# One triangular substitution for four delta-rule heads, heads run in two groups of four, and an order maker that repeats its passes with mean times

## The chip, the cores and the metric

The kernel runs on one core of a Trainium2 chip. Its time is that of one execution on the device, in microseconds. A core has five engines with instruction streams of their own: TensorE (PE; its weight loads are listed as PEld), VectorE (DVE), ScalarE (ACT), GpSimd (POOL) and SyncE (SP), which here issues the DMA transfers. They wait for one another by semaphores.

## The reference

One layer of a trunk, then a last RMSNorm; 1 x 1024 frames of 1024 features, 256 memory tokens, all float32. The delta-rule branch has 8 heads of 128 and works in chunks:

```python
h = rmsnorm(x, norm_mix_g); proj = h @ w_in        # all heads' columns at once
# branch A, gated DeltaNet, per head and chunk:
gc = jnp.cumsum(g, axis=-1)
decay = jnp.exp(jnp.where(incl, gc[..., :, None] - gc[..., None, :], -jnp.inf))
kk = jnp.einsum('bhnid,bhnjd->bhnij', k, k)
lower = jnp.where(strict, beta[..., :, None] * kk * decay, 0.0)
sol = triangular_solve(lower, [beta * v, beta * exp(gc) * k], lower=True, unit_diagonal=True)
a_qk = jnp.einsum('bhnid,bhnjd->bhnij', q, k) * decay
# scan over the chunks: delta = u - w S; o = q_dec S + a_qk delta; S = g_end S + k_dec^T delta
y_a = (rmsnorm(o) * silu(z)) @ w_branch_gdn
# branch B, GLA, 4 heads, gives y_b
x = x + (sigmoid(gate_a) * y_a + sigmoid(gate_b) * y_b) @ w_out
x = x + cross_attention(rmsnorm(x), rmsnorm(mem))  # 4 heads
x = x + relu(rmsnorm(x) @ w1)**2 @ w2
return rmsnorm(x, norm_final_g)
```

q, k and v pass a causal convolution of 4 taps and SiLU; q and k are l2-normalised.

## The kernel before

**Dense work.** Each float32 operand is split into a high and a low part (ScalarE rounds it, L622; VectorE or GpSimd subtracts, L623), and a product is made of three: high by high, high by low, low by high (L582, L584, L586). Large matrices go through a seven-product block scheme whose sums are the tiles A0a, A0b, A1a, A1b and B0a to B1b. One product has mostly 128 x 512 results. `wop`, `whi`, `wlo` are split weights and `raw` the weights as loaded.

**Phases.** First K and V of the memory, the norm of x (the factors `rs_o` are transposed at L679) and gates; then four GLA heads, between which the q, k, v columns of the delta-rule heads are projected, convolved (L1275) and stored in DRAM (`gd`, in the profile `gdq`, `gdk`, `gdv`, `gdz`); then the delta-rule phase; then gates, branch projections and merge, attention, MLP and the last norm.

**Delta-rule phase** (`phase_gdn`). The 8 heads run in 4 pairs. `near` loads a pair's k and, in `gdn_keys`, transposes it (L654, eight blocks for a head) for the norms and for `kd`, the keys times their decay (tile kdt, L1345). `gdn_decay` makes the matrix `dm` of a head from its cumulated gates: a load, a mask on GpSimd, a subtraction (L1326) and an exponential (L1327). `gdn_gram` multiplies k by itself (L1369) and makes `NT`, the negated strictly triangular matrix of a chunk. `gdn_subst` inverts its 32 x 32 diagonal blocks: ScalarE copies the blocks into the tile X (L1412), VectorE transposes (L1418), then 31 steps on VectorE or GpSimd make a product `pr` and add it to `Pm` (L1425, L1427), two transposes follow (L1429, L1431), and the results are copied to `PF` and `subPT`. X holds 32 columns; two heads of 8 blocks fill 16, the other 16 are set to zero. `gdn_inverse` joins the blocks to the inverse of the whole chunk on TensorE (L1449, L1458). `gdn_queries` makes q times k (L1386), `gdn_v` loads v and multiplies it (L1471), `gdn_scan` runs over the chunks (L1485, L1494, L1511) and writes its outputs over v, `gdn_out` transposes v (L654), multiplies by the SiLU of z (tile sz) and stores to `oad`. Pair p+1's keys, Gram products and substitution are written before pair p's scan. The v tiles of even and odd pairs have tags of their own (v0, v1), two buffers each.

**What fills and what orders.** Dense work (the z projections, numbered gates, the attention's folded weights Q0 to Q3 and O0 to O3) is pushed to a queue by `others(FILL[..])`, and `fill(n)` lets n of its steps into the program between steps of a head. But the order of the program is not the last word. The class `Plan` takes all instructions, gives each a cost, and makes a list schedule: `latest` works out by when each has to be done, `forward` places them; on TensorE the earlier in the program goes first of those that are ready, on other engines the one due earliest. Some operations may go to VectorE or GpSimd, as free. `make` repeats the two passes `ROUNDS` times (1 before) and keeps the order whose end is earliest by its own costs. `sooner(gen, SOON)` marks instructions as due SOON ns earlier. The buffers have fixed places (`LAYP`, `LAYQ`: tag, bytes, buffers).

Of the kernel before, what the change touches and what calls it, by code (L numbers as in the profile page):

```python
# [18 lines left out]
P = 128  # L19
D = 1024  # L20
T = 1024
NB = 8
# [18 lines left out]
FA, FB, FC, FD, FE, FG, FH, FI = 23, 31, 30, 20, 47, 24, 1, 0  # L41
# [6 lines left out]
EV = (('K2', 1, 'x0'), ('K3', 1, 'kk'), ('V0', 4, 'x1'), ('V1', 1, 's0'), ('V1', 12, 'n0'), ('V2', 12, 's1'), ('V3', 1, 'kv'), ('V3', 4, 'n1'))  # L48
# [18 lines left out]
EXTRA = (('k', 'v', 't', 'q'), ('v', 't', 'k', 'q'), ('v', 't', 'k', 'q'), ('v', 't', 'k', 'q'))  # L67
QB, FOLDB = 2, 1
SFILL, PFILL, TFILL = 4, (2, 12), (4, 14, 0, 8, 10, 10)
FILL = ((7,), ('z0', 6, 10, 'z6', 'Q2'), (9, 'O1', 'z5', 'Q3', 'z1'), ('z2', 'z4', 14, 'z3', 'O0', 11, 13, 'O3', 'Q0', 8, 'Q1'), ('z7', 'O2', 12))  # L70
LASTG = (15, 5)
LAYP = (('PF', 8192, 1), ('k1', 4096, 2), ('NT1', 4096, 2), ('NT0', 4096, 2), ('Pm', 4096, 1), ('dm', 4096, 2), ('k0', 4096, 2), ('kdt0', 4096, 2), ('kdt1', 4096, 2), ('pr', 1024, 1), ('q', 4096, 2))
LAYQ = (('AT', 4096, 2), ('v0', 4096, 2), ('acc', 2048, 2), ('sz', 2048, 2), ('v1', 4096, 2), ('X', 4096, 2))
OUT = "out_0_dram"
HOLD, MARGIN = 0, 0
SOON = 0
ROUNDS, TOP, PAD, WINDOW, LOAD, HORIZON, LAND, RATE = 1, 228656, 128, 3413, 1283, 30000, 2600, 300
# [100 lines left out]
class Plan:  # L178
# [252 lines left out]
    def make(self):  # L431
# [69 lines left out]
class Layer:  # L501
# [507 lines left out]
    def push_pair(self, sp, x, after=None):  # L1009
# [8 lines left out]
        def done(i, half, o, x_):  # L1018
            nc.scalar.activation(o, x_, AF.Silu)
            nc.sync.dma_start(self.gd["z", u][i][:, half * HALF:(half + 1) * HALF], o)  # L1020
# [171 lines left out]
    def queue_gla(self):  # L1192
# [5 lines left out]
        for h in range(LH):  # L1198
# [3 lines left out]
            q += [[a[f"w_g{x}"][h] if len(x) == 1 else a["w_gz"][int(x[1])]]  # L1202
# [132 lines left out]
    def gdn_keys(self, sp, sq, heads):  # L1335
# [3 lines left out]
        for e, (h, st) in enumerate(heads):  # L1339
            kd = st["kd"] = self.til(sp, [P, NB, P], f"kdt{h // 2 % 2}", bufs=2)  # L1340
            for g in range(2):
                gs = slice(4 * g, 4 * g + 4)
                pt = self.transpose4([st["k"][:, 4 * g + i, :] for i in range(4)])
                self.sumsq(sq, pt, ss[:, e, gs])
                nc.vector.tensor_tensor(kd[:, gs, :], c3(pt), self.kf[:, gs, h:h + 1].broadcast_to([P, 4, P]), MUL)  # L1345
                yield
        v, b, nb, vs = (self.til(sq, [P, 2, NB], t, bufs=2) for t in ("vv", "b", "nb", "vs"))
# [56 lines left out]
    def gdn_subst(self, sp, sq, sts):  # L1404
# [3 lines left out]
        nc.gpsimd.memset(C[:, :, 16:32], 0.0)  # L1408
# [22 lines left out]
        nc.vector.transpose(t2, Pm.rearrange("p i j -> p j i"))  # L1431

        PT, PF = self.subPT, self.til(sp, [P, 16, P], "PF", bufs=1)
        nc.gpsimd.memset(PF, 0.0)
        for b in range(4):
            q = slice(32 * b, 32 * b + 32)
            nc.scalar.activation(PF[q, :, q].rearrange("p u i -> p i u"), t2[q, :, 0:16], AF.Copy)
            nc.vector.tensor_copy(PT[q, :, q].rearrange("p u i -> p i u"), t1[q, :, 0:16])
# [130 lines left out]
    def phase_gdn(self, wp):  # L1569

        nc, a = self.nc, self.a
        with ExitStack() as ctx:
# [30 lines left out]
            def near(p):  # L1603
                for e, (h, st) in enumerate(heads(p)):
                    st["k"] = self.til(sp, [P, NB, P], f"k{p % 2}", bufs=2)
                    self.load(st["k"].rearrange("p a b -> p (a b)"), self.gd["k", p][e])
                yield from self.gdn_keys(sp, sq, heads(p))
# [9 lines left out]
            self.gdn_cols(sq)  # L1617
# [852 lines left out]
```

## Time and profile before

| what | value |
|---|---|
| median of 3 runs | 2115.37 us (2114.18 to 2116.24) |
| the profiled execution | 2115.5 us |
| its span in the profile | 2113.8 us |
| TensorE busy | 2091.5 us, 99% |
| VectorE busy | 1595.6 us, 75% |
| ScalarE busy | 1208.1 us, 57% |
| GpSimd busy | 152.2 us, 7% |
| delta-rule phase (first key transposes to last v transposes) | 673.8 to 1042.8 us |

The profile takes one execution. The busy time of an engine is the time in which it runs an instruction; matmuls are pipelined, so that each row of a matmul is longer than the spacing of two. Busy shares are means over stages with different limits: a stage is read from what its engines waited for. In a timeline, a row has start, duration, engine, line, operation, tiles and, in brackets, how long the engine had been idle and what released it. "x8" is a run of eight alike.

### The profile page before, as it was taken

The page shows a single profiled execution, that of the slowest core. Times are in us where ns is not written, and L with a number is a line of the kernel's source. Part 1 is how long each engine was busy: PE and PEld are TensorE (multiplying, and loading weights), DVE is VectorE, ACT ScalarE, POOL GpSimd, SP SyncE. Part 2 cuts the span into 40 slices and gives each one's busy share as a digit, 9 for nine tenths or more (in the row PEclk, how much of TensorE's full clock was granted, in tenths as well). Part 3 has the DMA queues.
Part 4 walks back from the last instruction along what each step waited for, and adds up shares of the span by engine and source line. Part 5 has one row for each costly group of instructions (what it writes and reads, how often), then busy time and mean ns, then how long its engine had stood idle before and what let it go on. Part 6 is the DMA issues. An engine that isn't in the chain of part 4 may idle for free. (4 is left out here: it accounts for less than half of the span.)

```text
span 2113.8 us, 30953 instructions
## 1 busy us (share of the span) xinstructions
PE 2091.5 (99%) x10938; PEld 1780.5 (84%) x10938; DVE 1595.6 (75%) x2830; ACT 1208.1 (57%) x2391; POOL 152.2 (7%) x174
## 2 busy tenths in 40 slices
PE   8999999999999999999999999999999999999998
PEld 8889887898888899889888888888788888888887
DVE  7858887948876888787569899469967567567855
ACT  7456666536646586765655456565755557444433
POOL 0000000001001223311000000000100000000000
PEclk9999999999999999999999999999999999999999
DMA  8322232312325444555586752226444446678852
GB/s 329 130 72 62 91 105 64 113 61 96 100 93 194 131 129 139 168 176 162 176 278 239 257 169 80 90 79 218 137 145 140 160 151 219 212 249 278 269 175 100
DMA packets 158363, 329.57 MB, mean 156 GB/s; under 512 B 17016, under 2 KB 25720, under 8 KB 158208
## 3 DMA queue, kind: packets, MB, share of 16 engines
q1 hardware_dynamic: 158064, 327.57, 47.1%
q8 instruction: 86, 1.41, 0.3%
q14 instruction: 69, 0.57, 0.1%
q10 hardware_dynamic: 144, 0.03, 0.0%
HBM read 227.36 MB, written 100.17 MB: 155 GB/s over the span
## 5 line engine op out<-in xcount | busy, mean ns | idle before, releaser
L622 ACT ACTIVATE wop<-raw 128x512 fp32r<-128x512 f32 (+1 forms) x520 | 336.6, 653 | 406.4 <-PE pd L586 179.5
L623 DVE TENSOR_TENSOR wop<-raw,wop 128x512 fp32r<-128x512 f32 (+1 forms) x494 | 347.3, 707 | 209.3 <-ACT wop L622 206.4
L582 PE MATMUL pd<-t,wop 128*128 128x512 f32 x332 | 130.4, 393 | 0.9 <-ACT t L622 0.9
L586 PE MATMUL pd<-t,wop 128*128 128x512 f32 x332 | 130.9, 394 | 0.0
L584 PE MATMUL pd<-t,wop 128*128 128x512 f32 x332 | 130.7, 394 | 0.0
L584 PE MATMUL pd<-A1b,wop 128*128 128x512 f32 x272 | 106.1, 390 | 0.0
L582 PE MATMUL pd<-A1b,wop 128*128 128x512 f32 x272 | 106.0, 390 | 0.0
L586 PE MATMUL pd<-A1b,wop 128*128 128x512 f32 x260 | 101.4, 390 | 1.4 <-DVE wop L623 1.4
L1275 DVE SCALAR_TENSOR_TENSOR dx<-dx,convw,dx 128x1023 f32<-128x1023 f32 (+2 forms) x72 | 90.3, 1277 | 2.2 <-ACT dx L1273 2.0
L582 PE MATMUL pd<-A1a,wop 128*128 128x512 f32 x208 | 81.6, 392 | 0.0
L584 PE MATMUL pd<-A1a,wop 128*128 128x512 f32 x208 | 81.5, 392 | 0.0
L586 PE MATMUL pd<-A1a,wop 128*128 128x512 f32 x196 | 76.7, 391 | 0.0
L582 PEld LDWEIGHTS pd<-t,wop 128*128 128x128 f32 x332 | 62.2, 188 | 14.5 <-ACT t L622 1.3
L584 PEld LDWEIGHTS pd<-t,wop 128*128 128x128 f32 x332 | 62.3, 188 | 13.2 <-DVE t L623 0.4
L586 PEld LDWEIGHTS pd<-t,wop 128*128 128x128 f32 x332 | 62.4, 188 | 12.8
L622 ACT ACTIVATE whi<-raw 128x512 fp32r<-128x512 f32 x70 | 43.0, 628 | 34.3 <-PE pd L584 15.2
L582 PEld LDWEIGHTS pd<-A1b,wop 128*128 128x128 f32 x272 | 51.1, 188 | 10.6 <-ACT wop L622 0.3
L584 PEld LDWEIGHTS pd<-A1b,wop 128*128 128x128 f32 x272 | 51.1, 188 | 10.4
L586 PEld LDWEIGHTS pd<-A1b,wop 128*128 128x128 f32 x260 | 48.8, 188 | 11.9 <-DVE wop L623 1.9
L623 DVE TENSOR_TENSOR wlo<-raw,whi 128x512 fp32r<-128x512 f32 x65 | 44.0, 685 | 17.7 <-ACT whi L622 17.7
L940 DVE TENSOR_TENSOR dx<-pd,dx 128x512 f32<-128x512 f32 x51 | 35.0, 687 | 16.9 <-PE pd L586 16.7
L582 PEld LDWEIGHTS pd<-A1a,wop 128*128 128x128 f32 x208 | 39.0, 188 | 8.3 <-ACT dx L935 0.3
(645 smaller groups left out, 6497.0 us busy)
## 6 DMA issues: line engine op xcount, KB each, us to landing
raw<-in_w_dram SPq DMA_DIRECT2D x120, 256.0 KB, 3.8
raw<-in_w_dram SPq DMA_DIRECT2D x32, 512.0 KB, 3.8
e<-ad SPq DMA_DIRECT2D x63, 256.0 KB, 4.7
ad<-q SPq DMA_DIRECT2D x45, 256.0 KB, 2.7
rawa<-ad SPq DMA_DIRECT2D x42, 256.0 KB, 4.6
A0b<-tgd SPq DMA_DIRECT2D x32, 256.0 KB, 5.2
ad<-acc SPq DMA_DIRECT2D x30, 256.0 KB, 2.3
ad<-u SPq DMA_DIRECT2D x30, 256.0 KB, 2.6
```

The lines of the kernel that those rows point to most:

```text
L582: nc.tensor.matmul(out, lh, rh, start=first and i == 0, stop=False, skip_group_check=True)
L584: nc.tensor.matmul(out, lh, rl, start=False, stop=False, skip_group_check=True)
L586: nc.tensor.matmul(out, ll, rh, start=False, stop=last and i == n - 1, skip_group_check=True)
L622: nc.scalar.activation(hi, raw, AF.Copy)
L623: (lo_eng or nc.gpsimd).tensor_tensor(lo, raw, hi.bitcast(F32), SUB)
L940: nc.vector.tensor_tensor(o, pt, o, ADD)
L1275: self.nc.vector.scalar_tensor_tensor(y[:, d:], x[:, :T - d], cw[:, 3 - d:4 - d], y[:, d:], MUL, ADD)
```

## The change

**Four heads in one substitution.** `gdn_subst` takes the NT of four heads (no zero columns), runs twice instead of four times, and returns two tiles; `gdn_unpack` copies a pair's half to PF and subPT when that pair's inverse is due. **Groups.** Pairs 0 and 1 are prepared before the first substitution, pairs 2 and 3 before the second. The key preparation of pair 3 runs beside the scan of pair 0 with its k in the place of PF, which is free then; pair 3's k is loaded and transposed a second time for `kd` (`gdn_turned`). The `dm` of pairs 1 and 3 is made twice, since only two buffers exist (12 instead of 8). **Buffers.** NT has three tags, v has one tag for all pairs (two buffers). **The order maker** runs 8 rounds, each starting from the mean of the times before and those just made, and SOON is 40000. The tables of what fills where (FILL, RFILL, EXTRA, LASTG, EV, FA to FI) have new numbers. A second form of gate weights is prepared on the host and not read.

```diff
-SFILL, PFILL, TFILL = 4, (2, 12), (4, 14, 0, 8, 10, 10)
+RFILL = ((8, 6, 8, 6), (8, 8, 5), (9, 8, 10, 8, 8, 5), (8, 12, 8, 0, 5), (8, 8, 8, 5, 12))
-LASTG = (15, 5)
+LASTG = (15,)
-SOON = 0
-ROUNDS, TOP, PAD, ... = 1, 228656, 128, ...
+SOON = 40000
+ROUNDS, TOP, PAD, ... = 8, 228656, 128, ...
...
             start, order = self.forward(deps, self.latest(deps, at, max(at) + 5000))
-            at, end = start, max(start)
+            at, end = [(x + y) / 2 for x, y in zip(at, start)], max(start)
...
+    def gdn_turned(self, sp, sq, heads, ss, kd):
         for e, (h, st) in enumerate(heads):
-            kd = st["kd"] = self.til(sp, [P, NB, P], f"kdt{h // 2 % 2}", bufs=2)
+            if kd:
+                st["kd"] = self.til(sp, [P, NB, P], f"kdt{h // 2 % 2}", bufs=2)
             for g in range(2):
                 pt = self.transpose4([st["k"][:, 4 * g + i, :] for i in range(4)])
...
-            NT = st["NT"] = self.til(sp, [P, NB, P], f"NT{h // 2 % 2}", bufs=2)
+            NT = st["NT"] = self.til(sp, [P, NB, P], f"NT{(0, 1, 0, 2)[h // 2]}", bufs=2)
...
         C = self.til(sq, [P, 32, 32], "X", bufs=2)
-        nc.gpsimd.memset(C[:, :, 16:32], 0.0)
...
+    def gdn_unpack(self, sp, ts, half):
+        (t1, t2), u = ts, slice(16 * half, 16 * half + 16)
...
-        v = st["v"] = self.til(sp, [P, NB, P], f"v{u % 2}", bufs=2)
+        v = st["v"] = self.til(sp, [P, NB, P], "v", bufs=2)
...
+            def both(p):
+                yield from self.gdn_qnorm(sq, heads(p))
+                r = self.til(sp, [P, 2, NB, P], "PF", bufs=1)
+                keys(3, [r[:, e] for e in range(2)])
+                decay(3)
+                yield from self.gdn_keys(sp, sq, heads(3), False)
+                yield from self.gdn_gram(sp, heads(3))
...
+            near(0, f[0])
+            decay(1)
+            near(1, f[1])
+            gram(1, f[2])
+            decay(0)
+            gram(0, f[3])
+            ts = self.gdn_subst(sp, sq, sts[0] + sts[1])
+            queries(0, f[0])
+            invert(0, ts, f[1])
+            scan(0, both(0), f[2], 2)
...
+            decay(1)
+            near(2, f[0])
+            queries(1, f[1])
+            decay(2)
+            gram(2, f[2])
+            invert(1, ts, f[3])
+            out(0, f[4])
+            ts = self.gdn_subst(sp, sq, sts[2] + sts[3])
+            scan(1, self.gdn_qnorm(sq, heads(1)), f[5])
...
+            keys(3)
+            run(self.gdn_turned(sp, sq, heads(3), None, True), f[0])
+            queries(2, f[1])
+            invert(2, ts, f[2])
+            out(1, f[3])
+            scan(2, self.gdn_qnorm(sq, heads(2)), f[4])
```

The order that results is shown at two places of the delta-rule phase and one before it. Numbers behind a name tell buffers apart; line numbers after the change are shifted (L1485 is L1501, L1494 is L1510, L1471 is L1487, L1275 is L1278, L1176 is L1179).

SP's queue at the load of pair 1's v, before:

```order
L541 DMA raw_7924<-in_wqT_dram 128x512
L541 DMA raw_7962<-in_wqT_dram 128x512
L1589 DMA gdz_114<-acc_7882 128x512
L541 DMA v_1383_8231<-gdv_109 128x1024
L541 DMA v_1384_8234<-gdv_109 128x1024
L541 DMA raw_7966<-in_wqT_dram 128x512
L541 DMA k_1196_7358<-gdk_111 128x1024
L541 DMA q_7354<-gdq_108 128x1024
```

and after:

```order
L541 DMA raw_9119<-in_wo_dram 128x512
L541 DMA v_8164<-gdv_109 128x1024
L541 DMA sz_7984<-gdz_106 128x512
L1563 DMA oad_70<-PF_7947 128x512
L541 DMA v_8167<-gdv_109 128x1024
L541 DMA sz_8013<-gdz_106 128x512
L541 DMA raw_9123<-in_wo_dram 128x512
```

The two v loads stood together, ahead of loads for the next pair; now they stand among the output stage's own transfers (sz is what z gives, oad what the stage stores), and the second stands behind a store of that stage.

TensorE at the start of pair 1's scan, before: the output stage of pair 0 transposes the old v tiles, and the scan's first product with the new v (L1494) follows.

```order
L586 MATMUL pd_8040<-A1a_204,wlo_8003 128x512
L654 MATMUL ps_8071<-ident_183,v_1021_6873 128x128 x4
L654 MATMUL ps_8079<-ident_183,v_1021_6873 128x128 x4
L654 MATMUL ps_8087<-ident_183,v_1022_6876 128x128 x4
L654 MATMUL ps_8095<-ident_183,v_1022_6876 128x128 x4
L1494 MATMUL ps_8251<-v_1383_8231,NT_954_6552 128x128
L586 MATMUL pd_8650<-A0a_202,wlo_8641 128x512
L582 MATMUL pd_8650<-A0b_203,whi_8640 128x512
```

and after, where the scan's first product with v_8164 (L1510) comes 24 dense products behind the last transpose:

```order
L654 MATMUL ps_7950<-ident_183,v_6785 128x128 x4
L654 MATMUL ps_7970<-ident_183,v_6785 128x128 x4
L654 MATMUL ps_7986<-ident_183,v_6788 128x128 x4
L654 MATMUL ps_8015<-ident_183,v_6788 128x128 x4
L584 MATMUL pd_8830<-A1b_5892,whi_8769 128x512
L586 MATMUL pd_8830<-A1b_5892,wlo_8770 128x512
```

The new tile v_8164 stands in the buffer of v_6785, so its load waits for the first two of these rows; before, the buffers were different ones.

VectorE in the second GLA head, from the convolution's taps to the operation that TensorE's transposes wait for (ex, L1176), before:

```order
L1275 SCALAR_TENSOR_TENSOR dx_3410<-dx_3362,convw_194,dx_3410 128x1023
L1275 SCALAR_TENSOR_TENSOR dx_3390<-dx_3279,convw_194,dx_3390 128x1021
L1275 SCALAR_TENSOR_TENSOR dx_3410<-dx_3362,convw_194,dx_3410 128x1022
L623 TENSOR_TENSOR wop_3456<-raw_3345,wop_3456 128x512
L1275 SCALAR_TENSOR_TENSOR dx_3410<-dx_3362,convw_194,dx_3410 128x1021
L1760 TENSOR_TENSOR raw_3345<-raw_3346,raw_3345 128x4x128
L1077 SCALAR_TENSOR_TENSOR ex_3222<-ex_3214,ex_3222 128x1024
L875 SCALAR_TENSOR_TENSOR ex_3230<-ones_190,ex_3222 128x128
L1176 SCALAR_TENSOR_TENSOR ex_3289<-ps_3291,cols_192,dx_2947 128x512
L1176 SCALAR_TENSOR_TENSOR ex_3290<-ps_3298,cols_192,dx_2948 128x512
```

and after:

```order
L1278 SCALAR_TENSOR_TENSOR dx_3410<-dx_3362,convw_194,dx_3410 128x1023
L1278 SCALAR_TENSOR_TENSOR dx_3390<-dx_3279,convw_194,dx_3390 128x1021
L1278 SCALAR_TENSOR_TENSOR dx_3410<-dx_3362,convw_194,dx_3410 128x1022
L1820 TENSOR_TENSOR raw_3345<-raw_3346,raw_3345 128x4x128
L1278 SCALAR_TENSOR_TENSOR dx_3410<-dx_3362,convw_194,dx_3410 128x1021
L1080 SCALAR_TENSOR_TENSOR ex_3256<-ex_3248,ex_3256 128x1024
L623 TENSOR_TENSOR wop_3460<-raw_3345,wop_3460 128x512
L875 SCALAR_TENSOR_TENSOR ex_3264<-ones_190,ex_3256 128x128
L1179 SCALAR_TENSOR_TENSOR ex_3299<-ps_3301,cols_192,dx_2947 128x512
L1179 SCALAR_TENSOR_TENSOR ex_3300<-ps_3308,cols_192,dx_2948 128x512
```

One split of a weight tile (L623) moved behind the last tap; the row of wop_3456, which stood among the taps, is now ahead of them.

More of the change, by code (lines that the diff above doesn't have):

```diff
@@ L1615, in run, with near, gram, queries @@
                     self.fill(n)
[L1617 to L1625 removed]
+            def near(p, n):
+                keys(p)
+                run(self.gdn_keys(sp, sq, heads(p)), n)
+            def gram(p, n):
+                run(self.gdn_gram(sp, heads(p)), n)
+            def queries(p, n):
                 for e, (h, st) in enumerate(heads(p)):
@@ L1658, in phase_gdn @@
+            f = RFILL[4]
+            others(FILL[4])
+            decay(3)
+            queries(3, f[0])
+            invert(3, ts, f[1])
+            out(2, f[2])
+            scan(3, self.gdn_qnorm(sq, heads(3)), f[3])
+            self.fill(f[4])
+            out(3, 2)
+            self.gdn_sums(sq, 3, heads(3))
             self.drain()
```

99 lines of the change are left out of this document (50 added, 49 removed).

## The prediction

> **What bounds the kernel now.** I read four views in turn: the page's busy times, busy time by stretches, the list of what TensorE waited for, and the timeline around each such wait. First the page.
>
> ```profile
> span 2113.8 us, 30953 instructions
> PE 2091.5 (99%) x10938; PEld 1780.5 (84%) x10938; DVE 1595.6 (75%) x2830; ACT 1208.1 (57%) x2391; POOL 152.2 (7%) x174
> ```
>
> TensorE is busy in 2091.5 of 2113.8 us, so 22.3 us are all that a better order can win while the work stays the same. VectorE and ScalarE count only where TensorE waits for them. Stretches of 50 us (columns: PE, PEld, DVE, ACT, POOL, then the granted clock) show the delta-rule phase, a dense phase and the end.
>
> ```profile
> 700.00:750.00 50.00, 48.75 (x295) 42.80 (x295) 43.12 (x101) 28.46 (x52) 14.01 (x17) 1.00 0.46 143
> 1850.00:1900.00 50.00, 50.00 (x222) 41.42 (x221) 32.47 (x50) 21.03 (x35) 1.58 (x1) 1.00 0.80 249
> 2100.00:2150.00 50.00, 6.08 (x31) 4.78 (x30) 10.39 (x28) 3.19 (x9) 2.41 (x3) 0.95 0.20 73
> ```
>
> The dense stretch runs 222 products in 50.00 us without a gap, so a 128x512 product costs 50/222 = 0.225 us. The clock is full in both. While the first substitution runs VectorE is at 43.12 of 50, and TensorE loses 1.25 us there. The list of waits says for what (total, times, longest):
>
> ```profile
> PE pd L582 <- ACT mT L736: 6.2, 2, 5.5
> PE pd L582 <- ACT q L935: 1.9, 2, 1.7
> PE pd L586 <- DVE wlo L623: 1.8, 2, 1.2
> PE ps L654 <- DVE ex L1176: 1.6, 1, 1.6
> PE pd L586 <- DVE wop L623: 1.4, 1, 1.4
> PE pd L582 <- ACT t L622: 0.9, 1, 0.9
> PE ps L1369 <- DVE kdt L1345: 0.4, 1, 0.4
> ```
>
> The first row is the start, before any operand is there; the others sum to 8.0 us. Of the remaining 22.3 - 14.2 = 8.1 us, the last stretch holds 13.8 - 6.1 = 7.7, the closing norm and store, which no edit touches. So the change cannot win more than 8.0 us (0.38%), and only those two rows that lie in the delta-rule phase, wlo and kdt (1.8 + 0.4 = 2.2), are waits for the work that it shortens. It can lose without such a limit.
>
> **The change, part by part.** *Products on TensorE.* Pair 3's keys are transposed a second time: 2 heads x 8 = 16 transposes more, nothing less. Here is a batch of eight and its follower, and the group of all of them.
>
> ```profile
> 673.79 1.06 PE L654 MATMUL ps<-ident,k 128*128 128x128 f32 x8
> 674.61 0.48 PE L586 MATMUL pd<-A0b,wlo 128*128 128x512 f32 x1
> ...
> L654 PE MATMUL ps<-ident,k x64: 270/272/301, 673.8 to 890.4; 128*128 128x128 f32 x64
> ```
>
> Eight take 674.61 - 673.79 = 0.82 us from start to start, 0.10 each; sixteen cost **+1.6**. If none overlapped they would cost 16 x 0.272 = 4.4, the upper bound. I take 1.6, the spacing of this very batch. All of it is on the path, since TensorE has no slack to hide it.
>
> *The substitution.* The triangular steps (tile pr, on VectorE and GpSimd) and the work around them:
>
> ```profile
> 660.00:740.00 80.00, 20.81 (x55) 3.17 (x7) 1.00 0.56 189
> 740.00:1080.00 340.00, 55.56 (x161) 13.75 (x25) 1.00 0.51 167
> sum 420.00, DVE 76.36 POOL 16.92; mean DVE 38.18 POOL 8.46
> ...
> L1418 DVE STREAM_TRANSPOSE X<-X x4: 1230/1239/1246, 695.8 to 919.3; 128x1024 f32<-128x1024 f32 x4
> ...
> L1429 DVE STREAM_TRANSPOSE X<-Pm x4: 1235/1246/1246, 737.4 to 960.7; 128x1024 f32<-128x1024 f32 x4
> ...
> L1431 DVE STREAM_TRANSPOSE X<-Pm x4: 1978/2042/2065, 738.6 to 962.7; 128x1024 f32<-128x1024 f32 x4
> ...
> L1326 DVE TENSOR_TENSOR dm<-dm,tm x8: 1208/1211/1990, 678.3 to 902.9; 128x1024 f32<-128x1024 f32 x8
> ...
> 735.56 0.50 PE L586 MATMUL pd<-A0a,wlo 128*128 128x512 f32 x1 [1.18 <-DVE wlo L623]
> ```
>
> The tile keeps its 32 columns (half were zeros), so a step costs what it did, 76.36 / 216 = 0.354 us, and VectorE has 122 of them now: 94 x 0.354 = 33.3 us less. Two rounds fewer save 2 x (1.24 + 1.25 + 2.04) = 9.1 of transposes; four more decay matrices add 4 x 1.21 = 4.8. VectorE is relieved by 37.6 us. That lies beside TensorE's products; on the path it is worth at most the waits above, of which the last row shows the longest. I take both of its kinds as gone, **-2.2** (0 at worst, if the relief falls elsewhere). ScalarE's extra decay exponentials are hidden: it is 57% busy. The six extra loads stand on queues that are about half used here (0.46 to 0.56 of the DMA engines in the rows).
>
> *The value tiles.* Pair p's v had a buffer of its own parity and was requested long ahead. Now all pairs share two buffers, so the load of pairs 1, 2 and 3 is issued only when the output stage of the pair before has transposed the tile away. On SP everything behind that load waits with it (the loads of sz and of w_o, in the rows of SP's order); waiting for the load are the multiply by beta (L1471) and the scan's first product. TensorE's order leaves eight transposes and 24 products between the release and that product: 8 x 0.10 + 24 x 0.225 = 6.2 us. Landing times (median, at the end of each row) and the multiply:
>
> ```profile
> raw<-in_w_gv_dram SPq DMA_DIRECT2D x8, 512.0 KB, 3.5
> dm<-gcd SPq DMA_DIRECT2D x8, 512.0 KB, 4.2
> v<-gdv SPq DMA_DIRECT2D x8, 512.0 KB, 5.8
> q<-gdq SPq DMA_DIRECT2D x8, 512.0 KB, 8.1
> ...
> L1471 DVE TENSOR_TENSOR v<-v,vs x8: 1211/1216/1219, 686.2 to 953.9; 128x1024 f32<-128x1024 f32 x8
> ```
>
> 6.2 - 1.2 leaves 5.0 for the landing. At 4.2 or below nothing waits; at 5.8 TensorE loses 0.8 per pair; at 8.1, 3.1 per pair. I take v's own row: 3 x 0.8 = **+2.4** (0 to 9.3; no gain, since the load waited for nobody before).
> [...]
>
> *Query tiles of pair 3.* The scan's last use of a q tile releases the load; the first query product needs it.
>
> ```profile
> 962.99 0.39 PE L1485 MATMUL ps<-S,q 128*128 128x128 f32 x2
> ...
> 967.96 0.49 PE L1386 MATMUL ps<-q,k 128*128 128x128 f32 x3
> ```
>
> That was 5.0 us without a wait. By the products between them the new order leaves 3.9, so the load, which took at most 5.0, costs 0 to 1.1; **+0.5**.
>
> *The first inverse.* From the last Gram product on which the first substitution rests to the first inverse product, TensorE had
>
> ```profile
> 683.52 1.05 PE L1369 MATMUL ps<-k 128*128 128x128 f32 x8
> ...
> 744.53 1.70 PE L1449 MATMUL ps<-PF,NT 128*128 128x96 f32 x14
> ...
> L1412 ACT ACTIVATE X<-NT x32: 635/652/677, 690.3 to 917.6; 32x256 f32<-32x256 f32 x32
> ```
>
> 744.5 - 684.3 (after the eight products) = 60.2 us of other work. In the new order it is worth 227 products of 0.225 and 16 query products of 2.28/19 = 0.12: 53.0 us. And eight more copies of 0.65, 5.2 us, stand in the chain. The chain's own parts sum to far less: 16 x 0.65 copies, 4.5 of transposes, (76.36 + 16.92) / 4 = 23.3 of steps, and at most 5 of copies back, 43 us. I take 0; if before was exactly filled, it is 7.2 + 5.2 = 12.4.
>
> *The order elsewhere.* Dense work moves too.
>
> ```profile
> 48.81 1.05 PE L679 MATMUL ps<-ident,rs_o 128*128 128x128 f32 x8
> ...
> 57.85 0.40 PE L582 MATMUL pd<-A0a,wop 128*128 128x512 f32 x1
> ...
> 360.60 1.07 PE L654 MATMUL ps<-ident,dx 128*128 128x128 f32 x6 [1.57 <-DVE ex L1176]
> ...
> 1485.11 7.01 POOL L623 TENSOR_TENSOR B1b<-q,B1b 128x512 fp32r<-128x512 f32 x1 [68.74 <-ACT B1b L622]
> ...
> 1492.15 0.60 ACT L935 ACTIVATE q<-pd 128x512 f32<-128x512 f32 x1 [3.13 <-POOL B1b L623]
> ```
>
> In the first 60 us, 13 products of 256 columns fewer (half of 0.225 each, 1.5 us in all) stand between the norm's factors and the first product that uses them, of 9.0 us; **+0.3** (0 to 1.5). The wait for ex stays: the ten VectorE rows before it are the same kinds in another order. The wait of ScalarE's q eviction stays: a 7.01 us split sits on GpSimd in both orders. At the end of the delta-rule phase the cover of the last output stage is by count 3.5 us shorter, where no wait is listed today; 0 (0 to 3.5).
>
> **Sum:** 1.6 - 2.2 + 2.4 + 0.5 + 0.3 = +2.6. The profiled execution took 2115.5 us, so 2118.1; the median of the runs lies 0.1 under it: **2118.0 us**, +0.12%. About 0.2% (4.2 us) is what a measurement of this kernel can tell from no change, so this counts as the same.
>
> **The rivals.**
>
> *Faster: the repeated passes clear the waits of the whole kernel.* With mean times over eight passes the order maker could remove every wait outside the start, and leave v enough time: 2115.5 + 1.6 - 8.0 = 2109.1. To be under 2111.3 it must take 5.8 of the 8.0. For it: passes that look ahead should see a 1.6 us hole. Against it: the rows around the two largest are unchanged in kind. Chance 0.22.
> [...]
>
> *Slower: v becomes the bound of each scan's start.* If the load lands like q's, at 8.1 us, each of three pairs loses 3.1: 2115.5 + 0.2 + 9.3 = 2125.0, with 0.2 = 1.6 - 2.2 + 0.5 + 0.3. It decides from a landing of 5.0 and is beyond 0.2% from 5.0 + 4.0/3 = 6.3. For it: v's median is nearer 6.3 than 4.2. Against it: 5.8 was measured with loads of k and q beside it, where now the smaller sz loads stand. Chance 0.27.
>
> *Slower: the first inverse is late.* Half of the 12.4 above, 2118.1 + 6.2 = 2124.3. Against it is the 43 us chain. Chance 0.07.
>
> **How the numbers follow.** The forecast has 0.44; its terms let it reach 2115 to 2120, so 0.02 of it counts as slower. Faster 0.22, same 0.42, slower 0.27 + 0.07 + 0.02 = 0.36. The range goes from the faster rival's 2109 to the v rival with the relief of 2.2 not realised, 2127; outside are a landing beyond 8.1 and a late inverse on top.
>
> **What would show it.** Right: TensorE's waits list has rows for the multiplied v at the scan's first product, two or three of about 1 us; the kdt and wlo rows of the delta-rule phase are gone; the ex and q rows remain at about 1.6 and 1.9; the landing of v<-gdv is 5 to 6; VectorE's busy time is near 1558. Wrong: no row for v and a sum of waits under 10 points to the faster rival; rows for v of 3 us each, or one of more than 4 us at the first inverse product, to the slower ones. A new wait at a place that I did not price, such as the output stages or the second substitution, would make the sum itself wrong.

## The result: slower by 0.68%

The changed kernel took 2129.33 us (median of 4 runs, 2126.96 to 2132.61) against 2114.86 before: a ratio of 1.0068, interval 1.0057 to 1.008. In a second series it was 1.0061 (1.0049 to 1.0074). The forecast was 2118.0, no change that could be told, and its range ended at 2127. The profiled execution took 2126.96, its span is 2125.3, so the two profiles differ by 11.5 us.

The changed kernel's page, its span and busy times:

```profile
span 2125.3 us, 30919 instructions
PE 2099.1 (99%) x10954; PEld 1786.0 (84%) x10954; DVE 1570.2 (74%) x2734; ACT 1223.1 (58%) x2403; POOL 134.8 (6%) x140
```

TensorE stood idle for 2125.3 - 2099.1 = 26.2 us, 3.9 more than before, and was busy 7.6 us longer. Its waits (total, times, longest):

```profile
PE pd L582 <- ACT mT L736: 5.5, 1, 5.5
PE ps L654 <- DVE ex L1179: 4.7, 1, 4.7
PE ps L1465 <- ACT PF L1453: 2.8, 1, 2.8
PE pd L584 <- DVE wop L623: 1.2, 2, 1.1
PE pd L586 <- DVE wlo L623: 0.9, 3, 0.4
```

The first row is the start. The two next are one hole each: the transposes of dx in the second GLA head, which wait for ex (1.6 us before, with a wait of 1.4 for a weight split shortly ahead of it), and the first inverse, where before had none. What comes behind these holes is seen in short stretches (columns: PE, PEld, DVE, ACT, POOL, then the granted clock):

```profile
360.00:362.00 2.00, 0.00 (x0) 0.00 (x0) 2.00 (x4) 1.30 (x3) 0.63 (x1) 1.00 0.00 0
362.00:364.00 2.00, 1.61 (x8) 1.64 (x9) 2.00 (x4) 0.42 (x1) 0.67 (x1) 0.55 0.81 259
364.00:366.00 2.00, 2.00 (x12) 1.96 (x11) 2.00 (x6) 2.00 (x6) 0.00 (x0) 0.60 1.01 391
...
764.00:766.00 2.00, 1.40 (x8) 1.43 (x9) 1.50 (x3) 1.95 (x3) 0.00 (x0) 0.74 0.07 16
766.00:768.00 2.00, 2.00 (x12) 2.00 (x11) 0.00 (x0) 1.20 (x3) 0.29 (x1) 0.50 0.72 247
768.00:770.00 2.00, 2.00 (x18) 2.00 (x18) 0.26 (x1) 1.93 (x4) 0.59 (x2) 0.91 0.39 138
```

The first row is the end of the first hole; the second hole ends at 764.6. From the end of each on the granted clock is 0.50 for 3.41 us (from 362.19 and from 764.96 us). Half a clock is not idle time: it hides in the busy time (in the stretch from 364 us TensorE is busy for 2.00 of 2.00 us at a clock of 0.60). It costs 2 x 0.45 + 2 x 0.40 = 1.7 us behind the first hole and 2 x (0.26 + 0.50 + 0.09) = 1.7 behind the second; a stretch at half clock is called a dip from here on. In before's profile no stretch of 2 us had a clock under 0.97 until TensorE's last product.

So the 11.5 us divide like this. The ex hole: 4.66 - 1.44 - 1.57 + 1.7 = 3.4. The first inverse: 2.76 + 1.7 = 4.5. The 16 new transposes: 1.8 (from start to next start, summed over the four groups). Together 9.7. The other 1.8 is not in the waits: those that are left (q and kdt gone, wlo halved, the start shorter, some short ones new) sum to 0.5 us less than before (26.2 - 22.3 - 1.65 - 2.76). It is in the busy time, which grew by 2.4 us more than the dips and the transposes explain (7.6 - 3.4 - 1.8). The small products grew most: from start to next start, without the waits, all 128 x 128 products took 143.8 us against 137.4 (144.0 in a second profile), with 1.8 of that for the new transposes. Why they take longer among the other work of the new order was not tried.

The landing of v, and the substitution's steps (tile pr, both stretches):

```profile
v<-gdv SPq DMA_DIRECT2D x8, 512.0 KB, 4.8
```

```profile
sum 420.00, DVE 44.02 POOL 0.83; mean DVE 22.01 POOL 0.42
```

VectorE's steps fell from 76.4 to 44.0 us, as the change means them to, and v landed in a median of 4.8.

### The profile page after: what moved, and what is told of

The parts are those of the page before. It is cut to its first block, busy times and chain, and to the rows that moved or that the text cites. A ratio compares the mean times of both kernels' runs of the same rounds, so it can differ in the third digit from the quotient of the medians.

```text
span 2125.3 us, 30919 instructions
## 1 busy us (share of the span) xinstructions
PE 2099.1 (99%) x10954; PEld 1786.0 (84%) x10954; DVE 1570.2 (74%) x2734; ACT 1223.1 (58%) x2403; POOL 134.8 (6%) x140
## 4 chain that ended last, share of the span: by engine, by line
PE 83%; DVE 10%; DMA 3%; issue 2%; ACT 2%; SPq 0%; DVEq 0%; ACTq 0%
PE pd L586 19%; PE pd L582 19%; PE pd L584 19%; PE ps L582 5%; PE ps L584 5%; PE ps L586 5%; PE ps L654 2%; DVE wop L623 2%; PE ps L1474 2%; DVE dx L1278 1%; PE ps L1465 1%; PE ps L1510 1%; PE ps L1398 1%; PE ps L1381 1%; PE ps L1527 1%
## 5 line engine op out<-in xcount | busy, mean ns | idle before, releaser
L623 DVE TENSOR_TENSOR wop<-raw,wop 128x512 fp32r<-128x512 f32 (+1 forms) x495 | 350.7, 711 | 211.4 <-ACT wop L622 209.8
L1278 DVE SCALAR_TENSOR_TENSOR dx<-dx,convw,dx 128x1023 f32<-128x1023 f32 (+2 forms) x72 | 91.2, 1290 | 2.6 <-ACT dx L1276 2.5
L623 DVE TENSOR_TENSOR wlo<-raw,whi 128x512 fp32r<-128x512 f32 x67 | 45.6, 686 | 23.3 <-ACT whi L622 22.1
L935 ACT ACTIVATE dx<-pd 128x512 f32<-128x512 f32 x51 | 30.1, 593 | 27.8 <-PE pd L586 24.6
```

Of the source, the lines that this page charges most:

```text
L623: (lo_eng or nc.gpsimd).tensor_tensor(lo, raw, hi.bitcast(F32), SUB)
L935: nc.scalar.activation(dest(*b), pt, AF.Copy, scale=scale)
L1278: self.nc.vector.scalar_tensor_tensor(y[:, d:], x[:, :T - d], cw[:, 3 - d:4 - d], y[:, d:], MUL, ADD)
```

## The experiments

Kernels named a_ start from the changed kernel, b_ from the kernel before. In a_ex, a_inv, a_both, a_ex2, a_inv2, a_both2, b_ex2 and b_best the order maker's result is kept and single rows of it are moved by hand; the others let it make an order anew. Lines in their profiles are shifted by the code that moves the rows. Ratios are to before, run on the same chip in the same series.

### Does the loss repeat, and is it the two holes?

The changed kernel again (after_again). 

> The changed kernel once more, as the base of the other runs of this call. Theory A (two holes and the clock): the loss of 11.5 us of span is mainly two holes in TensorE's stream that before did not have in this size, the wait for ex in the second GLA head (4.66 us) and the wait at the first inverse (2.76 us), each followed by some 4 us at half of the clock (1.7 us lost each). Its profile then shows the same two holes again, with granted clock near 0.5 behind them, and a time of 2127 to 2133. Theory B (spread): the loss lies in many small waits that change from execution to execution; then the holes differ in place and size between the two profiles.

Measured: 2129.37 us (1.0061, interval 1.0049 to 1.0074). The second profile has the same holes, 4.66 and 2.25 us, but a dip behind the first alone, and there it lasts twice as long, 6.8 us in place of 3.4; behind the second the clock (the column of 1.00) is full:

```profile
361.10:364.51 3.41, 2.67 (x13) 2.70 (x14) 3.41 (x7) 1.49 (x4) 1.01 (x1) 0.50 0.71 246
364.51:367.93 3.42, 3.42 (x12) 2.84 (x11) 3.20 (x7) 1.67 (x4) 0.00 (x0) 0.50 0.96 368
...
764.00:766.00 2.00, 0.97 (x9) 1.00 (x9) 1.85 (x4) 1.98 (x2) 0.00 (x0) 1.00 0.00 0
766.00:768.00 2.00, 2.00 (x21) 2.00 (x19) 0.00 (x0) 1.93 (x5) 0.60 (x3) 1.00 0.80 238
```

Both profiles so lose 3.4 us to dips, in different places. The holes are the order's (theory A); how long a dip follows, and whether one does, differs from one execution to the next.

What a gap costs, by itself (gaps, one run), 30 stretches of products with chains of copies between:

```diff
+for rep in range(3):
+    for m in range(1, 11):
+        for i in range(90 + 5 * rep + m):
+            nc.tensor.matmul(ps[i % 2], w, y, start=True, stop=True)
+        for i in range(m):
+            z = ys[1] if y is ys[0] else ys[0]
+            nc.vector.tensor_copy(z, ps[0] if i == 0 else y.bitcast(F32))
+            y = z
```

> A kernel of its own, which leaves out all of the reference's work: three times ten stretches of 91 to 110 products of 128x512 (some 20 to 25 us), each ended by a chain of 1 to 10 copies on VectorE that TensorE waits for (about 0.9 to 6.5 us). It measures what an idle gap of a given length costs in granted clock behind it. If the gate looks at the length of the gap alone, there is one length above which every gap is followed by a dip, somewhere between 1.6 and 2.2 us; if it looks at fixed windows of time, gaps of 2 to 4 us are followed by a dip in some of the three repeats and not in others, gaps under 1.5 never, gaps over 5 always.

The timeline gives each gap in brackets:

```profile
97.91 0.50 PE L2472 MATMUL pt<-y,w 128*128 128x512 f32 x1 [2.01 <-DVE y L2475]
...
639.43 0.50 PE L2472 MATMUL pt<-y,w 128*128 128x512 f32 x1 [2.01 <-DVE y L2475]
```

The same gap of 2.01 us was followed by half a clock at 98 us and by the full one at 639. Over the 29 gaps that have a whole stretch of products behind them: of nine between 0.56 and 1.71 us none had a dip; of six between 2.01 and 2.63 three had; of fourteen from 2.93 up all had. A dip made the next stretch 1.4 to 2.8 us longer than its number of products explains.

So it isn't the length alone. The trace's clock shows what it is: every dip behind a gap of this run lasts 3.41 us or twice that, and starts a whole multiple of 3.41 us after the first one, as if time were ruled into windows of 3.41 us. Here are the two gaps of 2.01 us on that ruling (PE's busy time is the second number, the clock the one of 1.00 or 0.50):

```profile
95.11:98.53 3.42, 1.41 (x7) 0.86 (x6) 1.97 (x4) 0.00 (x0) 0.00 (x0) 1.00 0.00 0
98.53:101.94 3.41, 3.41 (x10) 2.64 (x9) 0.00 (x0) 0.00 (x0) 0.00 (x0) 0.50 0.00 0
637.79:641.20 3.41, 1.77 (x8) 1.46 (x9) 1.41 (x4) 0.00 (x0) 0.00 (x0) 1.00 0.00 0
641.20:644.62 3.42, 3.42 (x17) 2.83 (x16) 0.00 (x0) 0.00 (x0) 0.00 (x0) 1.00 0.02 5
```

The first gap lies whole in one window, and the next window has half the clock. Of the second, 1.6 us lie in one window and 0.4 in the one before. Behind the first stretch of products, every window of this run at full clock with 1.95 us or more of idle time was followed by a dip, and none with 1.71 or less.

In every profile here that has more than one dip they stand on such a ruling, placed differently in each execution: the two dips of the changed kernel's first profile start 402.77 us apart, 118 times 3.413. That settles the two profiles above: the hole of 2.76 us (761.84 to 764.60) lay inside one window (761.55 to 764.96), the one of 2.25 was cut into 1.1 and 1.2. It also shows that short waits add up. Three waits near 1323 us (0.2, 0.5 and 1.05 us in the changed kernel) are split by a window's edge in both of its profiles, and no dip follows; in a_ex, a_inv, a_both, a_inv2 and a_both2 below they fall into one window with 1.6 to 1.7 us of idle time, and a dip follows. So from 1.6 to 1.9 us both happen, and two dips, in b_soon and a_sub2, follow windows with only 1.0 and 1.2 us; those stay open.

### Taking the holes away

The ex hole: the transposes behind 12 products of the changed order (a_ex).

```diff
 PE   L586 pd_3516<-A1b,wop_3456
-PE   L654 ps<-ident,dx x16
 PE   pd_3470<-t,wop_3453 x12
+PE   L654 ps<-ident,dx x16
 ACT  L1046 dx_3410 x2 / L622 wop_3464
+ACT  L935 dx_3483<-pd_3470 / L935 dx_3529<-pd_3516
 ACT  L1055 dx_3390<-ps_3417
```

> The order of the changed kernel kept row by row, but for one place: the 16 transposes that wait for ex in the second GLA head go behind the next 12 dense products, and two evictions on ScalarE that these products need go ahead of the eviction of those transposes. Theory A: the hole falls from 4.66 to about 4.66 - 12 x 0.225 = 1.95 us, which is near the 1.57 that left the clock alone before, so the clock stays at 1.00 there: 2.7 + 1.7 = 4.4 us less than the changed kernel. If the clock has nothing to do with the hole: 2.7 less, and the dip stays. Theory B: under 1 us, since the work that follows waits instead.

Measured: 2129.56 us against 2129.37 for the changed kernel, so nothing was gained. Its waits:

```profile
PE pd L603 <- ACT dx L956: 5.0, 3, 4.1
```

The products waited in the transposes' place: they need a pd tile that an eviction on ScalarE (dx, L956) empties; the longest wait for it was 4.1 us, since it stood behind a SiLU that waits for VectorE. The expectation failed on a queue that I had not followed.

The same with that eviction ahead of the SiLU, and one split later on VectorE (a_ex2).

```diff
+ACT  L935 dx_3483<-pd_3470
 ACT  L1046 dx_3410 x2
...
-DVE  L623 wop_3460
 DVE  L1179 ex x2
+DVE  L623 wop_3460
```

> The changed kernel's order row by row, but at the ex hole: the 16 transposes go behind 12 dense products (as in a_ex), the eviction that the first of those products waited for there goes ahead of the second SiLU of dx on ScalarE, and one weight split goes behind two of the evictions that make ex on VectorE. Theory A (hole and clock): the 12 products now run while VectorE works, the hole of 4.7 us falls to 1.4 to 2.0 us and the half clock behind it (1.7 us) goes: 4.5 us less than the changed kernel, 2124 to 2126. Theory S (VectorE's total): VectorE is behind TensorE there whatever the order, a new wait takes the place; under 1.5 us less.

Measured: 2127.26 us (1.0051, 1.0039 to 1.0064), 2.1 less than the changed kernel by the two ratios; span 2122.9, and no stretch of 2 us under a clock of 0.97 before TensorE's last product. From its waits:

```profile
PE pd L608 <- ACT dx L961: 2.7, 3, 1.9
...
PE pd L608 <- ACT wop L648: 2.2, 2, 1.7
```

The 4.66 became 1.9 ahead of the products, 0.5 for ex, 0.4 for another eviction and, ten us later, 1.7 for a weight split on ScalarE whose weights VectorE had prepared late: 4.5 in all. The idle time stayed, in smaller pieces, and the dip went. Theory S is right about the idle time and theory A about the clock. The two intervals overlap, so the gain of 2.1 is not clear of noise.

The first inverse: the decay matrices of pair 3 out of the steps (a_inv).

```diff
-DVE  L1329 dm_7036, dm_7043   (between the steps)
+DVE  the same, behind the first inverse
-ACT  L1330 dm_7036, dm_7043
+ACT  the same, behind the first steps of scan 0
```

> The order of the changed kernel kept row by row, but for the decay matrices of pair 3: their two subtractions on VectorE (1.2 us each), which stand among the first substitution's steps, and their two exponentials on ScalarE go behind the first inverse. Theory A: the chain to the first inverse is 2.4 us shorter, the hole of 2.76 us falls to about 0.3, the clock keeps 1.00: 2.4 + 1.7 = 4.1 us less than the changed kernel. If the chain was held by something else (the wait for the first decay matrix, the copies on ScalarE): no difference in the hole.

Measured: 2133.86 us (1.0085, 1.0072 to 1.0099), 4.5 more than the changed kernel. From its waits:

```profile
PE ps L1535 <- ACT dl L1530: 2.7, 1, 2.7
PE ps L1483 <- ACT PF L1471: 2.1, 1, 2.1
```

The hole stayed at 2.1, where the changed kernel's second profile had 2.25. Of the 2.4 us taken out, VectorE spent 0.90 on a wait for a weight split's other half, and the steps with their first transpose took 33.4 us against 34.7 and 34.1 in the changed kernel's two profiles; the first transpose began at 724.4 us, there at 723.1 and 724.1. So a part was gained and did not reach the hole in full. The two exponentials made a new hole of 2.7 us in the scan, with a dip; another dip, near 1331 us, is that of the three short waits and not the edit's. Both edits together (a_both): 

> Both edits together. Theory A: 4.4 + 4.1 = 8.5 us less than the changed kernel, some 4 us above before, and no clock under 0.95 between 10 and 2100 us. Theory B: well under that, 0 to 4 us.

Measured: 2134.25 us (1.0084, 1.007 to 1.0098), the holes of both, with four dips.

The transpose that PF needs first (a_inv2).

```diff
+nc.vector.transpose(t2, Pm.rearrange("p i j -> p j i"))
 nc.vector.transpose(t1, Pm)
-nc.vector.transpose(t2, Pm.rearrange("p i j -> p j i"))
...
-ACT  L1305 acc_7862   (ahead of the copies to PF)
+ACT  the same, behind them
```

> The changed kernel's order, but at the ends of the two substitutions VectorE makes the transpose that PF is copied from ahead of the other one, and one dense eviction on ScalarE goes behind the copies to PF. Theory A: the chain to the first inverse ends 1.2 us earlier, its hole falls from 2.2 to 2.8 to 1.0 to 1.6 us, under the length that a dip follows: 1.2 us less in all executions and 1.7 to 2.7 more in those that had a dip there; 2126.5 to 2128.5. If ScalarE's copies wait for something else, no difference.

Measured: 2131.5 us (1.0072, 1.0059 to 1.0084), about 2 more than the changed kernel by the two ratios, whose intervals overlap. From its waits, and from SP's and ScalarE's timelines:

```profile
PE ps L1493 <- ACT PF L1485: 1.9, 1, 1.9
PE ps L1484 <- ACT PF L1472: 1.6, 1, 1.6
...
765.96 0.38 SPq L1321 DMA_DIRECT2D Gd<-acc  x1
766.43 0.91 SPq L554 DMA_DIRECT2D raw<-in_w_gate_dram  x2
...
770.34 0.63 ACT L635 ACTIVATE whi<-raw 128x512 fp32r<-128x512 f32 x1 [1.93 <-DMA raw<-in_w_gate_dram]
```

The hole did fall to 1.6, and the eviction that was put behind the copies held up the inverse's next stage for 1.9, by way of two queues. The store of what it evicts (Gd) now leaves SP at 765.96 instead of 760.64; the two weight loads behind it leave at 766.43 instead of 764.93; and on ScalarE the split that waits for the first of them stands ahead of the copy that the inverse needs. Both (a_both2): 

> Both of these. Theory A: the two gains add, 6 to 7 us less than the changed kernel, about 2122 to 2124, still some 6 us above before, by the 16 transposes (1.8) and small waits in the scans. Theory S: 2 us or less.

Measured: 2129.19 us (1.0062, 1.0049 to 1.0076): no gain over the changed kernel.

On the kernel before, where engines have room (b_ex2, the rows of a_ex2 without the one on VectorE). 

> The kernel before, its order row by row, with the edit of a_ex2 on TensorE and ScalarE alone. Its hole for ex was 1.57 us without a dip: theory A gives 1.6 us less than before, 0.07%, at the edge of what can be told; the wait of 1.44 us ahead of it stays.

Measured: 2114.62 us (0.9992, 0.9983 to 1.0001), 1.6 less, as expected, though the interval just includes no change.

With one subtraction moved to VectorE as well (b_best):

```diff
-POOL L623 B1b<-q,B1b   7.01 us
+DVE  L623 B1b<-q,B1b
```

> The kernel before, its order row by row, with the edit of b_ex2 (1.6 us less) and one subtraction of a split (B1b, 7.0 us on GpSimd) moved to VectorE, where the same operation takes 0.7: the wait of 1.7 us for the q eviction near 1490 us goes. Theory A: 1.6 + 1.7 = 3.3 us less than before, 0.16%. If VectorE has no room there: 1.6 less or a new wait there.

Measured: 2112.35 us (0.9984, 0.9976 to 0.9993), 3.4 less than before; 3.3 were expected. This is the fastest version that was run. Its list of waits:

```profile
PE pd L614 <- DVE wlo L651: 1.7, 2, 1.2
...
PE pd L610 <- ACT q L963: 1.1, 1, 1.1
```

No row for ex is left, and the wait of 1.7 for the q eviction behind GpSimd is gone; the 1.1 stands at the eviction ahead of it, where before had 0.2.

### Which part of the change makes the holes?

Before's numbers for the GLA stage (a_gla), and these with one pass (a_gla1).

```diff
-FA, FB, FC, FD, FE, FG, FH, FI = 19, 32, 30, 20, 48, 20, 2, 0
+FA, FB, FC, FD, FE, FG, FH, FI = 23, 31, 30, 20, 47, 24, 1, 0
-EXTRA = (('v', 't', 'k', 'q'), ...
+EXTRA = (('k', 'v', 't', 'q'), ...
-ROUNDS = 8    # a_gla1
+ROUNDS = 1
```

> The changed kernel with before's numbers for the first GLA stage (FA to FI, EV, EXTRA[0]); the delta-rule phase, the eight passes and SOON stay. Theory G: the new order of the GLA stage, not the four-head substitution, made the hole of 4.66 us and the dip behind it; then this hole is back at 1.4 + 1.6 us without a dip and the time falls by 3 to 4 us, to about 2126. Theory D: nearly all of the loss comes from the delta-rule phase; then it stays within 1.5 us of the changed kernel.

> As the run before, and one pass of the order maker instead of eight: up to the delta-rule phase this is before's order but for shifted line numbers, so what is left over before's time is the price of the delta-rule edits alone. Theory G: 3 to 4 us under the changed kernel, and a wait list like before's up to 600 us. Theory D: over 10 us above before all the same, lost between 660 and 1080 us and at the two holes near 1320 us.

Measured: a_gla 2127.32 us (1.0047, 1.0034 to 1.0061). The ex hole is 2.2 there, and a new one stands at 730 us; a dip follows each (from 358.9 and from 734.4 us):

```profile
PE pd L582 <- ACT whi L622: 4.4, 1, 4.4
PE ps L654 <- DVE ex L1179: 2.2, 1, 2.2
```

a_gla1 took 2151.67 us (1.0162, 1.0148 to 1.0175), with waits like before's up to 600 us and these behind:

```profile
PE ps L1465 <- ACT PF L1453: 4.2, 1, 4.2
PE ps L582 <- ACT B1b L622: 3.5, 2, 2.6
PE pd L582 <- ACT wop L622: 3.4, 3, 2.5
```

All of the change but the GLA numbers and the passes costs 35 us in one pass, with six dips; the eight passes take back 24 of them. Theory G holds for the length of the ex hole, though not for the dip, and theory D for most of the time.

The changed kernel with one pass (a_rounds1; ROUNDS = 1). 

> The changed kernel with one pass of the order maker. With before's GLA numbers one pass gave 24 us more than eight. If that is the passes' worth on the new program whatever the GLA numbers, it is about 2150 here as well; if the GLA numbers were made for the new program, under 2140.

Measured: 2132.41 us (1.0075, 1.0061 to 1.0089). With the new GLA numbers the passes are worth 1.5 to 3 us by the ratios, within the intervals, and not 24; the first inverse waits 5.7 us there. What the passes are worth depends on the GLA numbers.

For the ex hole the runs make a table (us waited for the weight split just ahead, and for ex):

| | one pass | eight passes |
|---|---|---|
| before's GLA numbers | 1.4 and 1.6 (before, b_soon, a_gla1) | 0 and 2.2 (b_om, a_gla) |
| the new GLA numbers | 1.4 and 3.2 (a_rounds1) | 0 and 4.7 (the changed kernel, a_soon0) |

The new numbers make the idle time longer, by 1.6 to 2.4 us; the eight passes, where they change the order, turn two waits into one.

SOON at 0 in the changed kernel (a_soon0). 

> The changed kernel with SOON at 0 as before, the rest as changed. If marking the inverses as due early makes the first inverse's neighbours late, the time falls by 2 us or more; if the mark is what keeps the scans fed, it rises by 5 us or more with larger holes at the inverses; theory P: within 3 us, with holes at other places of the same total.

Measured: 2130.33 us (1.0068, 1.0055 to 1.008), as the changed kernel; its holes are at other places (4.7 for ex again, 2.3 for a load of q, three dips).

The order maker's part on the old program (b_om), and the mark alone (b_soon).

```diff
-SOON = 0
+SOON = 40000
-ROUNDS = 1    # b_om only
+ROUNDS = 8
-at, end = start, max(start)    # b_om only
+at, end = [(x + y) / 2 for x, y in zip(at, start)], max(start)
```

> The kernel before with the order maker's part of the change alone: eight passes with mean times and SOON of 40000, its own groups, tables and substitution. Theory P (the groups cost): 2114 to 2119, within 0.2% of before. Theory O (the order maker costs): several us above before, 2120 or more, with a hole over 2 us that before did not have.

> The kernel before with SOON of 40000 alone, one pass. With the eight passes as well it was 7.6 us slower than before, while eight passes without SOON give before's order row for row. If the mark alone is the cause: 2121 or more. If it is the passes' repeated use of the mark: within 3 us of before.

Measured: b_om 2123.49 us (1.0039, 1.0026 to 1.0051); b_soon 2126.73 us (1.0054, 1.0042 to 1.0066). Passes without the mark leave the old program's order as it was, row for row. So the mark alone costs the old program 11 us; the passes seem to take 3 of these back, but the two intervals overlap. Theory P falls: the old program, with its own groups, loses 8 to 11 us by the order alone, where the changed kernel loses 13 to 14. b_om's waits:

```profile
PE ps L654 <- DVE ex L1176: 2.2, 1, 2.2
PE ps L654 <- DMA k<-gdk: 1.7, 1, 1.7
PE ps L1449 <- ACT PF L1437: 1.6, 1, 1.6
```

One substitution for four heads against two for two, in the new groups (a_sub2).

```diff
+nc.gpsimd.memset(C[:, :, 16:32], 0.0)
...
-ts = self.gdn_subst(sp, sq, sts[0] + sts[1])
+ts = self.gdn_subst(sp, sq, sts[0])
 ...
 invert(0, ts, f[1])
+ts = self.gdn_subst(sp, sq, sts[1])
```

(and the same for pairs 2 and 3.) 

> The changed kernel with its groups, tables and passes, but with four substitutions of two heads (half of X zero again), each as late as the pair's inverse allows: pair 1's behind pair 0's inverse, pair 3's behind pair 2's. The chain to the first inverse is then 8 copies of 0.65 us shorter. Theory H (the first inverse): its hole of 2.2 to 2.8 us and the dip that follows in some runs go: 2 to 4.5 us less, although VectorE has 33 us more to do. Theory D': four heads against two does not matter at the first inverse, since VectorE's steps there stand behind weight splits that keep TensorE's pace; the hole stays within 1 us, the time the same or longer by the splits that come late.

Measured: 2145.29 us (1.0132, 1.0118 to 1.0146), 15 more than the changed kernel by the two ratios (0.0071 of 2117). The hole at the first inverse is gone, as theory H says, and others, most between 819 and 950 us, take more than it gave. The first rows of its waits below those for ex and the start:

```profile
PE pd L582 <- ACT whi L622: 3.1, 2, 2.4
PE ps L1475 <- DVE NT L1480: 2.2, 3, 1.5
```

VectorE is 40 us busier in this kernel than in the changed one. In the new groups the version with four heads is the faster one by 15 us. Since the whole order was made anew, how much of that is the substitution's own is not shown.

## Why the prediction was wrong

**The transposes** (+1.6): 1.8 measured. Right.

**The substitution** (-2.2): the steps shrank by 32.3 us of VectorE's time against 33.3 forecast, though VectorE as a whole by 25.4 and not 37.6, while GpSimd has 17.4 us less to do. The two waits: kdt is gone, wlo fell from 1.8 to 0.9. The mechanism was right and worth about 1.3.

**The v tiles** (+2.4): no row for v among the waits. The row chosen for the landing was a mixed one: its median of 5.8 holds pair 0's two loads, which took 9.2 and 10.0 us among 9 to 11 other transfers. Here are the loads of pairs 1 to 3 alone, before and after:

```profile
DMA to landing us min/median/max: 4.1/4.9/6.6
DMA to landing us min/median/max: 3.8/4.7/7.1
```

Asked for late, v landed as it did before. The condition of 5.0 us held for the first head of a pair, whose product comes 6.2 to 6.3 us after the request; for the second head it comes 7.3 to 8.6 after, and so the slowest load, 7.1, cost nothing.

**The q tiles** (+0.5): nothing here, but 0.9 in a_gla and 2.3 in a_soon0 show the load to be that close.

**The first inverse** (0): this step failed. I summed the chain to 43 us, against 53 of cover; from the last Gram product (ends near 705) to the inverse it took 60, and TensorE had 56 us of other work. The rows show what the sum left out (start, duration, operation, what the engine waited for):

```profile
706.24 1.22 DVE L1329 TENSOR_TENSOR dm<-dm,tm 128x1024 f32<-128x1024 f32 x1 [2.32 <-POOL dm L1327]
...
712.61 2.16 DVE L1384 SCALAR_TENSOR_TENSOR NT<-ps,nb,dm 128x128 f32<-128x128 f32 x8
...
757.63 0.19 DVE L1438 TENSOR_TENSOR Pm<-Pm,pr 128x31 f32<-128x31 f32 x1
757.85 1.25 DVE L1440 STREAM_TRANSPOSE X<-Pm 128x1024 f32<-128x1024 f32 x1
759.02 2.07 DVE L1442 STREAM_TRANSPOSE X<-Pm 128x1024 f32<-128x1024 f32 x1
```

```profile
712.13 10.96 ACT L1423 ACTIVATE X<-NT 32x256 f32<-32x256 f32 x16
...
761.19 1.10 ACT L1453 ACTIVATE PF<-X 32x512 f32<-32x512 f32 x1 [0.58 <-DVE X L1442]
```

Pair 0's decay matrix is the last to be made, since two buffers serve two pairs, so NT ends at 714.8, ten us after the product. The copies end at 723.1 (11.0 against 10.4 summed). The steps then last until 757.8: 33.5 us against 23. Their own work is 22.1 of that, so this term was right as busy time; 6.6 more are eleven weight splits that stand between them, 2.3 two decay matrices and 2.6 idle time. The sum took VectorE's busy time for the time that passes. The prediction's own rows held the better number: before, the stretch from the end of the first transpose (695.8 + 1.2) to the next (737.4) took 40.4 us. a_inv shows that taking the decay matrices out brings 0.8 to 1.4 of their 2.4. The rival had a chance of 0.07 and the price of 6.2; measured were 2.8 and a dip of 1.7 in one profile, 2.25 and none in the other. So the rival with the lowest chance had the place right.

**"The wait for ex stays"**: this failed too. The rows ahead of it were the same kinds in another order, and that was taken to mean the same moment. Here is VectorE from the four taps to ex, before and after:

```profile
350.96 4.86 DVE L1275 SCALAR_TENSOR_TENSOR dx<-dx,convw,dx 128x1022 f32<-128x1022 f32 x4
359.72 2.70 DVE L1176 SCALAR_TENSOR_TENSOR ex<-ps,cols,dx 128x512 f32<-128x512 f32 x4
...
352.88 4.86 DVE L1278 SCALAR_TENSOR_TENSOR dx<-dx,convw,dx 128x1022 f32<-128x1022 f32 x4
361.52 2.70 DVE L1179 SCALAR_TENSOR_TENSOR ex<-ps,cols,dx 128x512 f32<-128x512 f32 x4
```

The rows took as long as before (8.6 us against 8.8), so the split that changed its place among them is not what made ex late: VectorE began them 1.9 us later, behind other work. TensorE, which had not waited for the split, arrived 1.3 us earlier, and the two short holes became one long one. The table of the GLA numbers puts the longer idle time on them: with before's numbers and eight passes it is 2.2 us.

**The clock.** No term had it. Holes were priced at their length; where some 2 us of idle time fell into one window of 3.41 us they cost 1.7 or 3.4 more in the changed kernel's two profiles. Of the 11.5 us, 3.4 are this.

**The rivals.** "The passes clear the waits" was the wrong way round for the new order as a whole, though by these runs the passes save 1.5 to 24 us. "v" didn't come about. The statement that was borne out is the prediction's last: a new wait at a place without a price makes the sum itself wrong.

What stays open: why the mark costs 11 us on the old program and nothing on the new, and the share of the groups in the new program's loss, since each edit made the planner give another order, and each order had its own holes. Of the seven orders that it made anew in these runs all were slower than before, by 0.39 to 1.62%. That the spread of the changed kernel's runs (2126.7 to 2132.6) comes from dips that fall in some executions agrees with the profiles and with the gaps, but no run showed it execution by execution. A difference of 2 us between two versions of the changed kernel can be this luck.

## What to carry to other kernels

Price a hole in TensorE's stream by its length, and add the 1.7 to 3.4 us that the half clock cost here where 2 us of idle time or more can fall into one of the windows of 3.41 us that these traces show; count short waits that stand within such a window together, as three waits with 1.6 to 1.7 us between them had a dip behind them in a_ex. Read the clock in stretches of 2 us, since a share of busy time hides it (2.00 of 2.00 us busy at a clock of 0.60). A chain on one engine takes the time that passes there, with the work that stands between its steps (33.5 us here), and not the sum of its own rows (22.1). Where a planner makes the whole order anew, a count of operations says little: the holes that were followed here sit where the orders of two engines meet (in a_inv2 ScalarE waited 1.93 us for a weight load, with the copy that the inverse needs behind it), and every wait must be followed through the order of the engine that ends it. Moving single rows of a good order gave what the wait rows promised where engines had room (1.6 us, at the edge of noise, and 3.4), and moved the wait elsewhere where VectorE or ScalarE was behind.

## What the hardware showed that was not expected

The granted clock of the one busy core fell from 1.00 to 0.50 for 3.41 us or 6.83 us, on a ruling of 3.41 us windows, behind a window that in the run gaps had 1.95 us or more of idle time; the same gap of 2.01 us cost 1.6 us of clock or nothing, by where a window's edge fell. By the gaps of that run: from 2.93 us a dip came every time (14 of 14), up to 1.71 never (0 of 9); in a_ex and four more runs three waits of 0.2 to 1.05 us in one window had one behind them too. A load of 512 KB that was asked for late, among four to seven other transfers, landed in a median of 4.7 us against 4.9 where it was asked for early.
